# A two-block decoder kernel: first loads in one queue, a forget bias spread through HBM, and a recurrence whose second token block runs backwards

## The chip, the cores and the metric

The kernel runs on one core of a Trainium2 chip. The metric is the device time of one execution, in microseconds. The time before is 1769.55 us, the median of three runs (1769.51 to 1770.18).

Engines are named as the profile names them: PE (TensorE matmul), PEld (its weight load), DVE (VectorE), ACT (ScalarE), POOL (GpSimd) and SP (SyncE, which issues most DMAs). Each engine works through its own instructions in order; an instruction that waits for another engine holds up all that stand behind it.

## The reference, cut to what matters

256 tokens of width 2048 go through two residual blocks. The first has a gated linear recurrence (8 heads, 128 keys) beside dilated attention, then a convolution-gated MLP; the second has a causal convolution, attention with a forget gate, and memory attention. Only the recurrence and the forget bias are touched:

```python
q = silu(q_raw); f = lbh + (1 - lbh) * sigmoid(f_raw)
k = 1 - f; logf = log(f); v = i_raw
# S_t = diag(f_t) S_{t-1} + (1 - f_t) outer i_t ; o_t = S_t^T q_t
...
cT = cumsum(logf, axis=1).transpose(0, 2, 1)      # forget gate of the second block
bias = ci[..., :, None] - cT[..., None, :]
s = where(mask, q @ k.T * scale + bias, -inf)
```

The recurrence can be written as causal scores: the score of query t and key s is the sum over the 128 keys of q_t k_s times the product of all f between s and t.

## The kernel before

All activations lie as [feature, token] tiles in SBUF. Every large product is done in two parts: a weight piece is rounded to fp32r by ACT (`hi`, L208) and the rest is taken by DVE (`lo`, L193), and PE multiplies hi with both parts of the activation (L324, 512 columns) and lo with the first part (L326, 256 columns). One such pair is the beat of the kernel. `fm` makes [feature, token] outputs of 512 features in two halves of 16 k-tiles, 32 pairs each; `tm` makes [token, feature] outputs in 16 steps of six 512-column products (L389 to L391). SP streams the weights in the order of one list; a `raw` buffer is free again when its `lo` is made, and four pieces are kept ready ahead of PE.

The order of the instructions is written out by hand. `step()` (L287) is called after every second k-tile of `fm` and every k-tile of `tm`: it first does what has ended (`flush`: the evacuation of a half, `evac`, L360, and for a second half its `then`, such as `forgets`), and then lets the generator in the lane run to its next `yield`. So each `yield` of `hgrn` (L428) puts four pairs of `fm` (or six products of `tm`) between two of its stages.

`hgrn` treats four heads at a time and both blocks of 128 tokens. For levels L = 1, 2, 4 to 64, neighbouring stretches of L tokens are joined: PE multiplies all 128 keys of a block with all 128 of its queries (L455, 4 heads x 2 blocks = 8 products of 128 columns in full fp32), `copy_predicated` (L472) takes from the result the queries of the second stretch of each pair against the keys of the first, DVE multiplies these queries by the decay of the first stretch (L463), the keys of the first stretch by the decay of the second (L465), and the decays with one another (L468, `tot`). Then L477 multiplies the keys of block 0 with the queries of block 1, and L488 to L491 apply the scores to the values.

`forget` (L1073) ends with a cumulative sum `lz` of 8 rows; L1126 spreads each row over 128 partitions with a selector matrix, 16 fp32r products in four groups, and ACT and DVE carry them to `nb0` and `nb1`.

At the start, ACT issues the small `vec` and the first four k-tiles of x (L684, three transfers), SP the weights and the rest of x (`queue_first`, L236). `first` (L692) scales a k-tile (L152, L153) and then fetches its weight piece.

Of the kernel before, what the change touches and what calls it, by code (L numbers as in the profile page):

```python
# [17 lines left out]
T = 256  # L18
# [20 lines left out]
C_TRI, C_CAUS, C_LNC, C_LV = 0, 128, 256, 640  # L39
NCONST = 640 + 64 * len(LEVELS)  # L40


def constants():
    c = np.zeros((128, NCONST), np.float32)
    i = np.arange(128)
    c[:, C_TRI:C_TRI + 128] = i[:, None] <= i[None, :]
# [7 lines left out]
    for n, L in enumerate(LEVELS):  # L54
        t = i[i // L % 2 == 1]
        c[:, C_LV + 64 * n:C_LV + 64 * (n + 1)] = (i[:, None] // (2 * L) == t // (2 * L)) & (i[:, None] // L % 2 == 0)
    return c
# [10 lines left out]
def body(ctx: ExitStack, tc: tile.TileContext, A: dict, out: bass.AP):  # L68
# [10 lines left out]
    pb = ctx.enter_context(tc.tile_pool(name="pb", bufs=4, space=bass.MemoryType.PSUM))  # L79

# [346 lines left out]

    def hgrn(hh):  # L428
        f, q, v = hst.pop((hh, "f")), hst.pop((hh, "q")), hst.pop((hh, "v"))
        k = G("hk")  # L430
# [4 lines left out]
        Q = G("hQ")  # L435
        dve.tensor_tensor(out=Q, in0=q, in1=f, op=ALU.mult)
        yield
        for b in range(2):
            sl = slice(b * 128, (b + 1) * 128)
            ps = PB("sc", (128, 4, 128))  # L440
            for h in range(4):
                pe.matmul(ps[:, h, :], lhsT=k[:, h, sl], rhs=q[:, h, sl], start=True, stop=True)
            yield
            dve.tensor_tensor(out=SD[:, b], in0=ps, in1=bc(ident, 4), op=ALU.mult)
        yield
        tot = f.rearrange("p h t -> p (h t)")
        kf = k.rearrange("p h t -> p (h t)")
        Qf = Q.rearrange("p h t -> p (h t)")
        for n, L in enumerate(LEVELS):
            ps = []  # L450
            for b in range(2):
                sl = slice(b * 128, (b + 1) * 128)
                ps.append(PB("sc", (128, 4, 128)))
                for h in range(4):
                    pe.matmul(ps[b][:, h, :], lhsT=k[:, h, sl], rhs=Q[:, h, sl], start=True, stop=True)  # L455
            yield
            m = cst[:, C_LV + 64 * n:C_LV + 64 * (n + 1)].bitcast(U32).rearrange("p (n l) -> p n l", l=L)
            m = m.unsqueeze(1).to_broadcast([128, 4, 64 // L, L])
            Qv = Qf.rearrange("p (n a l) -> p n a l", a=2, l=L)[:, :, 1, :]
            kv = kf.rearrange("p (n a l) -> p n a l", a=2, l=L)[:, :, 0, :]  # L460
            tv = tot.rearrange("p (n a) -> p n a", a=2)
            t0, t1 = tv[:, :, 0], tv[:, :, 1]
            dve.tensor_tensor(out=Qv, in0=Qv, in1=bc(t0, L, 2), op=ALU.mult)  # L463
            yield
            dve.tensor_tensor(out=kv, in0=kv, in1=bc(t1, L, 2), op=ALU.mult)  # L465
            if L < 64:
                nt = G("tot", (128, 512 // L))
                dve.tensor_tensor(out=nt, in0=t0, in1=t1, op=ALU.mult)  # L468
                tot = nt
            yield  # L470
            for b in range(2):
                dve.copy_predicated(out=SD[:, b].rearrange("p h (n a l) -> p h n a l", a=2, l=L)[:, :, :, 1, :], mask=m,  # L472
                                    data=ps[b].rearrange("p h (n a l) -> p h n a l", a=2, l=L)[:, :, :, 1, :])
# [207 lines left out]
    with tc.manual_schedule():  # L681
        act.dma_start(out=vec[:, 0:16], in_=A["vecs"][:, 0:16])
        for a, b in ((0, 1), (1, 2), (2, 4)):
            act.dma_start(out=hT[0][:, a:b, :], in_=A["xT"][:, a:b, :])  # L684
# [7 lines left out]
        def first(rhs, src, name):  # L692
# [16 lines left out]
            for k0, n in FIRST:  # L709
                for k in range(k0, k0 + n):  # L710
                    rhs[k // 4].put_scaled(k % 4, src[k // 4][:, k % 4, :], V("ln_mix_pre", k))
                held.append(next_piece())
# [32 lines left out]

        def forgets(hh):
            def then(z):
                times(z, rb1)
                act.activation(out=z, in_=z, func=AF.Sigmoid)
                for h in range(4):  # L750
                    c = 4 * hh + h
                    dve.tensor_scalar(out=z[:, h, :], in0=z[:, h, :], scalar1=omlb[:, c:c + 1], scalar2=lb[:, c:c + 1],
                                      op0=ALU.mult, op1=ALU.add)
# [7 lines left out]
        silu(zq)  # L761
        hg = []
        for hh in range(2):
            hst[hh, "f"] = fm(uT, "hf", forgets(hh)) if hh else zf
            hst[hh, "q"] = fm(uT, "hq", silu) if hh else zq
            zf = zq = None
            if hh == 0:
                r1 = row_to_col(rb1, "r1")
            hst[hh, "v"] = token_scaled(tm(uT), r1, "hv")
# [298 lines left out]
        sel = G("sel", (8, 1024))  # L1068
        pool.dma_start(out=sel, in_=A["sel"])

        nbias = {}

        def forget():  # L1073
# [5 lines left out]
            s8 = G("selr", (8, 1024), F32R)  # L1079
            act.copy(out=s8, in_=sel)  # L1080
# [33 lines left out]
            c = Parts("nc", (8, T))  # L1114
            c.put(lz)
            yield
            yield
            caus = cst[:, C_CAUS:C_CAUS + 128]
            for hh in range(2):
                b0, b1 = G("nb0", (128, 4, 128)), G("nb1")  # L1120
                for p in range(2):
                    ps = PB("nb", (128, 2, T))
                    for a in range(2):
                        h = 4 * hh + 2 * p + a
# [4 lines left out]
                    hs = slice(2 * p, 2 * p + 2)  # L1129
                    act.copy(out=b1[:, hs, 0:128], in_=ps[:, :, 0:128])  # L1130
                    dve.tensor_tensor(out=b0[:, hs, :], in0=ps[:, :, 0:128], in1=bc(caus, 2), op=ALU.add)
                    dve.tensor_tensor(out=b1[:, hs, 128:256], in0=ps[:, :, 128:256], in1=bc(caus, 2), op=ALU.add)
                    yield
# [73 lines left out]
        del zp, zc, cu, sel  # L1207
# [99 lines left out]
```

## Time and profile before

| | |
|---|---|
| median of three runs | 1769.55 us |
| the profiled execution, device time | 1769.86 us |
| its span, first to last instruction | 1768.1 us |
| mean granted PE clock | 0.998 |
| DVE busy | 1191.6 us (67%) |
| ACT busy | 926.6 us (52%) |
| DMA | 323.73 MB, 183 GB/s in the mean |

The profile's share of busy time for PE counts products as pipelined, so that a single product's duration is longer than the distance to the next. What a group of products costs on PE is therefore read from the distance between starts. A row of the timeline gives the start, the duration, engine, line, operation, tiles and the number of records; a full fp32 product has two records, so "x16" on L455 are 8 products. In square brackets stands the idle time of that engine just before the row, and what ended it.

### The profile page before, as it was taken

How to read it: one execution, taken by the hardware profiler on the slowest of the kernel's cores; microseconds unless marked ns; L12 is line 12 of the kernel's file. 1: busy time of each engine (PE TensorE's matmuls, PEld its weight loads, DVE VectorE, ACT ScalarE, POOL GpSimd, SP SyncE). 2: the span in 40 equal slices, each digit the busy share in tenths (PEclk: the TensorE clock that was granted, in tenths of full speed). 3: DMA queues.
4: the chain of work that ended last, by engine and by line, in shares of the span. 5: the costliest groups of instructions: out<-in, count | busy, mean ns of one | idle time of the engine just before them, and what ended most of it. 6: DMA issues, size and time to landing. Idle time of an engine off the chain costs nothing.

```text
span 1768.1 us, 24303 instructions
## 1 busy us (share of the span) xinstructions
PE 1755.6 (99%) x9508; PEld 1513.0 (86%) x9508; DVE 1191.6 (67%) x1503; ACT 926.6 (52%) x1237; POOL 4.6 (0%) x12
## 2 busy tenths in 40 slices
PE   9999999999999999999999999999999999999998
PEld 8898988888888888888888888888888888888886
DVE  6775655567777777777777764444777688787564
ACT  6534354556655555555555653443655455448543
POOL 0000000000000000000000000000000000000000
PEclk9999999999999999999999999999999999999999
DMA  8644445555655665555565556555465545554553
GB/s 296 204 142 155 143 156 177 184 198 191 197 185 190 190 191 189 188 190 189 191 190 188 184 190 211 192 192 190 155 191 192 170 160 169 175 172 161 177 192 126
DMA packets 234482, 323.73 MB, mean 183 GB/s; under 512 B 10168, under 2 KB 203192, under 8 KB 234368
## 3 DMA queue, kind: packets, MB, share of 16 engines
q1 hardware_dynamic: 232816, 318.22, 55.2%
q0 software_dynamic: 976, 3.44, 0.6%
q8 instruction: 74, 1.21, 0.3%
q10 hardware_dynamic: 576, 0.53, 0.1%
q14 instruction: 40, 0.33, 0.1%
HBM read 320.06 MB, written 2.10 MB: 182 GB/s over the span
## 4 chain that ended last, share of the span: by engine, by line
PE 99%; DMA 0%; DVE 0%; ACT 0%; ACTq 0%; issue 0%; DVEq 0%
PE fm L324 40%; PE fm L326 20%; PE tm L389 10%; PE tm L390 10%; PE tm L391 10%; PE sc L455 1%; PE as L574 1%; PE fm L704 1%; PE ao L564 0%; DMA hT<-in_xT 0%; PE bd L623 0%; PE tm L1256 0%; PE tm L1254 0%; PE tm L1255 0%; PE at L553 0%; PE fm L705 0%
## 5 line engine op out<-in xcount | busy, mean ns | idle before, releaser
L324 PE MATMUL fm<-uT,hi 128*128 128x512 f32 x2688 | 947.9, 397 | 0.0
L208 ACT CAST hi<-raw 128x1024 fp32r<-128x1024 f32 (+1 forms) x591 | 617.1, 1048 | 590.6 <-PE fm L324 261.0
L193 DVE TENSOR_TENSOR lo<-raw,hi 128x1024 fp32r<-128x1024 f32 (+1 forms) x591 | 715.2, 1218 | 198.2 <-ACT hi L208 197.4
L326 PE MATMUL fm<-uT,lo 128*128 128x256 f32 x2688 | 747.9, 278 | 0.0
L324 PEld LDWEIGHTS fm<-uT,hi 128*128 128x128 f32 x2688 | 504.3, 188 | 116.2 <-issue 0.4
L326 PEld LDWEIGHTS fm<-uT,lo 128*128 128x128 f32 x2688 | 505.9, 188 | 0.9
L389 PE MATMUL tm<-hi,gp 128*128 128x512 f32 x352 | 136.9, 389 | 0.0
L391 PE MATMUL tm<-hi,gp 128*128 128x512 f32 x352 | 136.9, 389 | 0.0
L390 PE MATMUL tm<-lo,gp 128*128 128x512 f32 x352 | 136.9, 389 | 0.0
L363 DVE TENSOR_TENSOR up<-fm,up 128x512 f32<-128x512 f32 x44 | 30.4, 692 | 90.2 <-ACT up L362 89.3
L324 PE MATMUL fm<-hP,hi 128*128 128x512 f32 x256 | 90.7, 399 | 0.0
L391 PEld LDWEIGHTS tm<-hi,gp 128*128 128x128 f32 x352 | 66.1, 188 | 13.9
L390 PEld LDWEIGHTS tm<-lo,gp 128*128 128x128 f32 x352 | 66.1, 188 | 13.7
L389 PEld LDWEIGHTS tm<-hi,gp 128*128 128x128 f32 x352 | 66.1, 188 | 13.6
L880 ACT ACTIVATE upc<-up,vec 128x256 f32<-128x256 f32 x88 | 52.7, 599 | 45.9 <-DVE up L406 45.9
L389 PE MATMUL tm<-hi,uT 128*128 128x512 f32 x192 | 75.5, 393 | 0.0
L390 PE MATMUL tm<-lo,uT 128*128 128x512 f32 x192 | 74.9, 390 | 0.0
L391 PE MATMUL tm<-hi,uT 128*128 128x512 f32 x192 | 74.8, 389 | 0.0
L326 PE MATMUL fm<-hP,lo 128*128 128x256 f32 x256 | 71.9, 281 | 0.0
L324 PEld LDWEIGHTS fm<-hP,hi 128*128 128x128 f32 x256 | 48.1, 188 | 11.8
L1027 DVE SCALAR_TENSOR_TENSOR conv<-ca,vec,conv 128x255 f32<-128x255 f32 (+14 forms) x120 | 55.7, 464 | 1.5
L883 DVE SCALAR_TENSOR_TENSOR upc<-up,vec,upc 128x255 f32<-128x255 f32 x88 | 42.3, 480 | 14.1 <-ACT upc L880 14.1
(309 smaller groups left out, 1802.6 us busy)
## 6 DMA issues: line engine op xcount, KB each, us to landing
raw<-in_w_in SPq DMA_DIRECT2D x215, 512.0 KB, 4.6
raw<-in_w_up SPq DMA_DIRECT2D x176, 512.0 KB, 4.4
raw<-in_w_down SPq DMA_DIRECT2D x88, 512.0 KB, 4.5
raw<-in_w_out SPq DMA_DIRECT2D x64, 512.0 KB, 4.6
raw<-in_w_pg SPq DMA_DIRECT2D x32, 512.0 KB, 4.4
raw<-in_w_mem_kv SPq DMA_DIRECT2D x16, 512.0 KB, 4.8
memt<-in_memT POOLq DMA_DIRECT2D x4, 512.0 KB, 6.3
raw<-in_w_pe SPq DMA_DIRECT2D x4, 512.0 KB, 4.3
```

Source lines behind the costliest of these rows:

```text
L193: dve.tensor_tensor(out=lo, in0=src, in1=f32(hi), op=ALU.subtract)
L208: act.copy(out=hi, in_=src)
L324: pe.matmul(ps[:, f, :], lhsT=hi[:, kk, fs], rhs=u.both(i), start=(done == 0), stop=False, skip_group_check=True)
L326: pe.matmul(ps[:, f, T:2 * T], lhsT=lo[:, kk, fs], rhs=u.hi(i), start=False, stop=(done == n_k - 1), skip_group_check=True)
L363: dve.tensor_tensor(out=o, in0=ps[:, :, 0:T], in1=o, op=ALU.add)
L389: pe.matmul(ps[:, t, :], lhsT=u.hi(i)[:, ts], rhs=hi[:, kk, :], start=(done == 0), stop=False)
L390: pe.matmul(ps[:, t, :], lhsT=u.hi(i)[:, ts], rhs=lo[:, kk, :], start=False, stop=False)
L391: pe.matmul(ps[:, t, :], lhsT=u.lo(i)[:, ts], rhs=hi[:, kk, :], start=False, stop=(done == n_k - 1))
L455: pe.matmul(ps[b][:, h, :], lhsT=k[:, h, sl], rhs=Q[:, h, sl], start=True, stop=True)
L880: act.activation(out=y[:, f, :], in_=s[:, f, :], func=AF.Identity, scale=V("conv_w", 176 + c), bias=V("conv_b", c))
L883: dve.scalar_tensor_tensor(out=y[:, f, 1:], in0=s[:, f, 0:T - 1], scalar=V("conv_w", 88 + c), in1=y[:, f, 1:], op0=ALU.mult, op1=ALU.add)
L1027: dve.scalar_tensor_tensor(out=c[:, f, sh:], in0=cu[:, f, 0:T - sh], scalar=w, in1=c[:, f, sh:], op0=ALU.mult, op1=ALU.add)
```

## The change

- **First loads.** The three x transfers of ACT's queue are gone. SP now issues: weight tile 0, x tiles 0 and 1, weight tile 1, x tiles 2 and 3, weight tiles 2 and 3, and so on. `first` fetches the weight pieces 0 and 1 before it scales their x tiles.
- **Recurrence.** f, q, k and Q lie as [block, head, token], and block 1 has its tokens reversed. X holds, per head, one 128-column operand with the keys of the first stretches of block 0 and the second (in time: also first) stretches of block 1; Y holds the others. A level multiplies X with 64 queries of each block: 4 products of 128 columns, with a right operand read in runs of L. After the product, ACT copies half of X from Y, and DVE makes the other half of X, `tot` and half of Y. One more `yield` stands ahead of the levels, with two ACT copies that build X and Y. The values of block 1 are reversed by three POOL transfers through HBM.
- **Forget bias.** The selector, its load and L1126 go. POOL writes `lz` to HBM, reads four rows at a time back to all 128 partitions, and after eight yields DVE adds the causal mask.

```diff
     def queue_first(w, c0):
         for k, n in FIRST:
-            if k in (4, 8, 12):
-                load_x(k, k + 4)
+            if k in (2, 4, 8, 12):
+                load_x(k, min(2 * k, k + 4))
...
+            if k == 0:
+                load_x(0, 2)
...
     def hgrn(hh):
...
+        scores = (SD[:, 0], SD[:, 1, :, ::-1])
...
+        X2, Y = G("hX", (128, 2, 512)), G("hY", (128, 512))
+        X = X2[:, 0]
+        act.copy(out=X.rearrange("p (n a) -> p n a", a=2), in_=strided(kf, 0, (2, 256), (513, 2)))
+        act.copy(out=Y.rearrange("p (n a) -> p n a", a=2), in_=strided(kf, 512, (2, 256), (-511, 2)))
+        del k, kf
+        yield
+        for e, (L, masks) in enumerate(zip(LEVELS, C_LV)):
+            ps = PB("sc", (128, 4, 2, 64))
+            for h in range(4):
+                pe.matmul(ps[:, h].rearrange("p b q -> p (b q)"), lhsT=X[:, h * 128:(h + 1) * 128],
+                          rhs=strided(Qf, h * 128 + L, (512 - L, 2), (2 * L, 64 // L), (1, L)), start=True, stop=True)
+            yield
+            N, S = 256 // L, 512 // L
+            Qv = strided(Qf, L, (512 - L, 2), (2 * L, N), (1, L))
+            dve.tensor_tensor(out=Qv, in0=Qv, in1=strided(tot, 0, (S + 1, 2), (2, N), (0, L)), op=ALU.mult)
+            yield
+            X1 = X2[:, 1 - e % 2]
+            if L < 64:
+                M = N // 2
+                same, other = ((4 * L, M), (3 * L, 2), (1, L)), ((4 * L, M), (L, 2), (1, L))
+                act.copy(out=strided(X1, L, *other), in_=strided(Y, L, *other))
+                dve.tensor_tensor(out=strided(X1, 0, *same), in0=strided(X, 0, *same),
+                                  in1=strided(tot, 1, (4, M), (S + 1, 2), (0, L)), op=ALU.mult)
...
             yield
...
         ps = PB("sc", (128, 4, 128))
         for h in range(4):
-            pe.matmul(ps[:, h, :], lhsT=k[:, h, 0:128], rhs=Q[:, h, 128:256], start=True, stop=True)
-        act.copy(out=SO, in_=ps)
+            pe.matmul(ps[:, h, :], lhsT=X[:, h * 128:(h + 1) * 128], rhs=Q[:, 1, h, :], start=True, stop=True)
+        act.copy(out=SO[:, :, ::-1], in_=ps)
...
         act.dma_start(out=vec[:, 0:16], in_=A["vecs"][:, 0:16])
-        for a, b in ((0, 1), (1, 2), (2, 4)):
-            act.dma_start(out=hT[0][:, a:b, :], in_=A["xT"][:, a:b, :])
...
+        def folded(z, func, name):
+            y = G(name, (128, 2, 4, 128))
+            act.activation(out=y[:, 0], in_=z[:, :, 0:128], func=func)
+            act.activation(out=y[:, 1], in_=z[:, :, 255:127:-1], func=func)
+            return y
...
         def forgets(hh):
             def then(z):
                 times(z, rb1)
-                act.activation(out=z, in_=z, func=AF.Sigmoid)
+                y = folded(z, AF.Sigmoid, "hf")
...
+            pool.dma_start(out=rows, in_=v[:, 1, :])
...
+            pool.dma_start(out=back.rearrange("t (a c) -> a t c", a=2),
+                           in_=rows[::-1, :].rearrange("t (a c) -> a t c", a=2))
+            pool.dma_start(out=v[:, 1, :], in_=back)
...
-                        for part in (c.hi, c.lo):
-                            pe.matmul(ps[:, a, :], lhsT=s8[:, 128 * h:128 * (h + 1)], rhs=part, start=(part is c.hi),
-                                      stop=(part is c.lo))
...
+            pool.dma_start(out=spread, in_=lz)
...
+                pool.dma_start(out=b1, in_=spread[4 * hh:4 * hh + 4, :].partition_broadcast(128))
+                for _ in range(8):
                     yield
```

Three places of the order matter for what follows. The first is DVE in the recurrence of the first four heads, around level 4, where the second half of the next f (`hf`) is evacuated (L363), scaled by the norm (L406) and turned into f (L752). Before:

```order
L463 TENSOR_TENSOR hQ<-hQ,tot 128x128x4
L465 TENSOR_TENSOR hk<-hk,tot 128x128x4
L468 TENSOR_TENSOR tot<-tot 128x128
L193 TENSOR_TENSOR lo<-raw,hi 128x1024
L363 TENSOR_TENSOR hf<-fm,hf 128x512
L406 TENSOR_TENSOR hf<-hf,rb 128x1024
L752 TENSOR_SCALAR hf<-hf,omlb,lb 128x256 x4
L472 COPY_PREDICATED SD<-cst,sc 128x64x4 x2
L193 TENSOR_TENSOR lo<-raw,hi 128x1024
```

The same place on DVE now (L367, L410 and L784 are the evacuation, the norm and f; L480 makes X):

```order
L473 TENSOR_TENSOR hQ<-hQ,tot 128x2x64x4
L195 TENSOR_TENSOR lo<-raw,hi 128x1024
L367 TENSOR_TENSOR hf<-fm,hf 128x512
L410 TENSOR_TENSOR hf<-hf,rb 128x1024
L784 TENSOR_SCALAR hf<-hf,omlb,lb 128x2x128 x4
L480 TENSOR_TENSOR hX<-hX,tot 128x32x2x4
L484 TENSOR_TENSOR tot<-tot 128x128
L485 TENSOR_TENSOR hY<-hX,tot 128x32x8
L497 COPY_PREDICATED SD<-cst,sc 128x64x4
L497 COPY_PREDICATED SD<-cst,sc 128x4x16x4
```

Before, the keys for level 8 (L465) stood ahead of the work on f; now X for level 8 (L480) stands behind it.

The second place is ACT at the end of the same recurrence, at level 64, where the second half of the next q (`hq`) gets its Silu and the last product's result is copied to SO. Before:

```order
L362 COPY hq<-fm 128x512
L758 ACT_TABLE_LOAD
L758 ACTIVATE hq<-hq 128x1024
L478 COPY SO<-sc 128x512
L208 CAST hi<-raw 128x1024 x2
```

Now (L479 and L489 are the copies from Y to X):

```order
L479 COPY hX<-hY 128x4x64
L210 CAST hi<-raw 128x1024 x2
L366 COPY hq<-fm 128x512
L774 ACT_TABLE_LOAD
L774 ACTIVATE hq<-hq 128x512
L775 ACTIVATE hq<-hq 128x512
L489 COPY hX<-hY 128x4x64
L210 CAST hi<-raw 128x1024
L503 COPY SO<-sc 128x4x128
```

A copy that the last product needs now stands behind the table load and the Silu.

The third place is SP's first DMAs. Before (row 1 is two transfers, and ACT's three x transfers go out beside them):

```order
L185 DMA raw<-in_w_in 128x512 x2
L185 DMA raw<-in_w_in 128x1024
L229 DMA hT_89<-in_xT 128x1024
L185 DMA raw<-in_w_in 128x1024 x2
L229 DMA hT_90<-in_xT 128x1024
```

Now:

```order
L187 DMA raw<-in_w_in 128x512
L231 DMA hT_90<-in_xT 128x512
L187 DMA raw<-in_w_in 128x512
L231 DMA hT_90<-in_xT 128x512
L187 DMA raw<-in_w_in 128x1024
L231 DMA hT_91<-in_xT 128x1024
L187 DMA raw<-in_w_in 128x1024 x2
```

All of x's first tiles stand in the one queue, each beside the weights that meet it.

## Rows read from the trace of the kernel before

**Rows 1.** The page's first part: busy time, share of the span and instructions of each engine.

```profile
PE 1755.6 (99%) x9508; PEld 1513.0 (86%) x9508; DVE 1191.6 (67%) x1503; ACT 926.6 (52%) x1237; POOL 4.6 (0%) x12
```

**Rows 2.** All waits of PE over the span: waiting engine and line, what it waited for, us in total, times, longest us. There are five; the three left out are one wait each of under 1.2 us, none of them in the recurrence.

```profile
PE fm L704 <- DVE uT L153: 1.9, 1, 1.9
...
PE fm L705 <- DVE lo L193: 0.6, 1, 0.6
```

**Rows 3.** The timeline of PE in the recurrence of the first four heads: start us, duration us, engine, line, operation. Between 81.47 and 83.77 lie four pairs of L324 and L326, between 89.57 and 94.43 fourteen, between 87.44 and 94.78 sixteen.

```profile
81.47 1.05 PE L442 MATMUL sc<-hq,hk 128*128 128x128 f32 x8
...
83.77 1.05 PE L442 MATMUL sc<-hq,hk 128*128 128x128 f32 x8
...
87.44 1.95 PE L455 MATMUL sc<-hQ,hk 128*128 128x128 f32 x16
...
89.57 0.40 PE L324 MATMUL fm<-uT,hi 128*128 128x512 f32 x1
...
94.43 0.39 PE L324 MATMUL fm<-uT,hi 128*128 128x512 f32 x1
...
94.78 1.95 PE L455 MATMUL sc<-hQ,hk 128*128 128x128 f32 x16
```

**Rows 4.** The timeline of PE at the first two groups of the forget bias; eight pairs lie between the groups, six of them between 1436.39 and 1438.51.

```profile
1435.28 0.73 PE L1126 MATMUL nb<-nc,selr 8*128 8x256 f32 x4
...
1436.39 0.39 PE L324 MATMUL fm<-uT,hi 128*128 128x512 f32 x1
...
1438.51 0.40 PE L324 MATMUL fm<-uT,hi 128*128 128x512 f32 x1
...
1438.95 0.74 PE L1126 MATMUL nb<-nc,selr 8*128 8x256 f32 x4
```

**Rows 5.** The first 12 us in stretches: its length, busy us (and instructions) of PE, PEld, DVE, ACT and POOL, granted PE clock, DMA share, GB/s.

```profile
0.00:4.00 4.00, 2.95 (x14) 2.95 (x15) 0.17 (x2) 1.36 (x2) 0.20 (x4) 1.00 0.34 78
4.00:6.00 2.00, 1.56 (x10) 1.37 (x9) 0.00 (x0) 0.11 (x1) 0.00 (x0) 1.00 1.01 369
6.00:8.00 2.00, 0.47 (x1) 0.19 (x1) 1.13 (x2) 1.01 (x2) 0.00 (x0) 1.00 1.02 406
8.00:10.00 2.00, 1.90 (x6) 1.70 (x7) 1.20 (x3) 1.02 (x2) 0.00 (x0) 0.56 1.04 395
10.00:12.00 2.00, 2.00 (x9) 1.67 (x8) 0.91 (x3) 1.86 (x4) 0.00 (x0) 0.59 1.03 414
```

**Rows 6.** The start of the chain that ended last: start us, us, what. The first row is the transfer of x tiles 2 and 3.

```profile
2.15 7.97 DMA hT<-in_xT
10.14 0.91 ACT uT L152 x2
...
12.02 1.24 DVE lo L193
```

**Rows 7.** The timeline of PE at the first product, at a later pair, and at the product that the last row of the group before releases.

```profile
7.48 0.47 PE L704 MATMUL fm<-uT,hi 128*128 128x512 f32 x1 [1.92 <-DVE uT L153]
...
9.02 0.63 PE L704 MATMUL fm<-uT,hi 128*128 128x512 f32 x1
...
9.66 0.63 PE L704 MATMUL fm<-uT,hi 128*128 128x512 f32 x1
...
13.30 0.38 PE L705 MATMUL fm<-uT,lo 128*128 128x256 f32 x1 [0.58 <-DVE lo L193]
```

**Rows 8.** The timelines of ACT, DVE and PE where the second half of `hf` ends, by engine.

```profile
110.40 1.06 ACT L749 ACTIVATE hf<-hf 128x1024 f32<-128x1024 f32 x1 [0.71 <-DVE hf L406]
...
111.49 1.38 DVE L752 TENSOR_SCALAR hf<-hf,omlb,lb 128x256 f32<-128x256 f32 x4 [1.12 <-ACT hf L749]
112.78 0.76 DVE L472 COPY_PREDICATED SD<-cst,sc 128x256 f32<-128x256 uint32 x2
...
109.54 1.95 PE L455 MATMUL sc<-hQ,hk 128*128 128x128 f32 x16
```

**Rows 9.** The same where the second half of `hq` ends: PE's first product of `tm` behind it and the product that stands 12 products later, and ACT's Silu.

```profile
136.21 0.39 PE L389 MATMUL tm<-hi,uT 128*128 128x512 f32 x1
...
138.98 1.05 PE L477 MATMUL sc<-hQ,hk 128*128 128x128 f32 x8
...
139.84 1.06 ACT L758 ACTIVATE hq<-hq 128x1024 f32<-128x1024 f32 x1 [0.72 <-DVE hq L406]
```

**Rows 10.** The same place as rows 8 for the other four heads, where the half is of `aq` and only scaled.

```profile
193.53 1.23 DVE L406 TENSOR_TENSOR aq<-aq,rb 128x1024 f32<-128x1024 f32 x1
...
193.94 1.95 PE L455 MATMUL sc<-hQ,hk 128*128 128x128 f32 x16
```

**Rows 11.** Durations of DVE and ACT work on 256 and 512 columns: a group of DVE by form (busy us, mean ns), the copies of ACT at L1130, and the multiply of the queries at levels 2 to 64 and at level 1 (ns min/median/max).

```profile
L468 DVE TENSOR_TENSOR tot<-tot 128x256 f32<-128x256 f32 x1 | 0.4, 417 | 0.0
...
L1130 ACT COPY nb<-nb x4: 352/364/374, 1436.5 to 1447.4; 128x256 f32<-128x256 f32 x4
...
L463 DVE TENSOR_TENSOR hQ<-hQ,tot x12: 683/692/694, 96.8 to 218.0; 128x512 f32<-128x512 f32 x12
L463 DVE TENSOR_TENSOR hQ<-hQ,hf x2: 693/694/695, 89.4 to 173.8; 128x512 f32<-128x512 f32 x2
```

**Rows 12.** POOL's transfers: size, us from issue to landing. `gf` is one row spread over 128 partitions.

```profile
gf<-in_final_g POOLq DMA_DIRECT2D x2, 512.0 KB, 5.2
...
sel<-in_sel POOLq DMA_DIRECT2D x1, 32.0 KB, 3.1
```

More of the change, by code (lines that the diff above doesn't have):

```diff
@@ L37 @@
 NVEC = _o
-C_TRI, C_CAUS, C_LNC, C_LV = 0, 128, 256, 640
-NCONST = 640 + 64 * len(LEVELS)
+C_CAUS, C_LNC = 0, 128
+C_LV = [(512 + 128 - 128 // L, 512 + 127 + 128 - 128 // L) for L in LEVELS]
+NCONST = 512 + 2 * 127
 def constants():
@@ L445, in hgrn @@
         yield
[L446 to L455, printed above, removed]
-            yield
[L457 to L463, printed above, removed]
+        tot = f.rearrange("p b h t -> p (b h t)")
@@ L467, in hgrn @@
                 nt = G("tot", (128, 512 // L))
-                dve.tensor_tensor(out=nt, in0=t0, in1=t1, op=ALU.mult)
+                tv = tot.rearrange("p (n a) -> p n a", a=2)
+                dve.tensor_tensor(out=nt, in0=tv[:, :, 0], in1=tv[:, :, 1], op=ALU.mult)
+                dve.tensor_tensor(out=strided(Y, L, *other), in0=strided(X, L, *other),
+                                  in1=strided(tot, S, (4, M), (3 - S, 2), (0, L)), op=ALU.mult)
                 tot = nt
+            else:
+                act.copy(out=strided(X1, 64, (128, 4), (1, 64)), in_=strided(Y, 64, (128, 4), (1, 64)))
+                dve.tensor_tensor(out=strided(X1, 0, (128, 4), (1, 64)), in0=strided(X, 0, (128, 4), (1, 64)),
+                                  in1=strided(tot, 1, (2, 4), (0, 64)), op=ALU.mult)
@@ L748, in then, with queries @@
                 times(z, rb1)
-                act.activation(out=z, in_=z, func=AF.Sigmoid)
+                y = folded(z, AF.Sigmoid, "hf")
                 for h in range(4):
                     c = 4 * hh + h
-                    dve.tensor_scalar(out=z[:, h, :], in0=z[:, h, :], scalar1=omlb[:, c:c + 1], scalar2=lb[:, c:c + 1],
-                                      op0=ALU.mult, op1=ALU.add)
+                    dve.tensor_scalar(out=y[:, :, h, :], in0=y[:, :, h, :], scalar1=omlb[:, c:c + 1],
+                                      scalar2=lb[:, c:c + 1], op0=ALU.mult, op1=ALU.add)
+                hst[hh, "f"] = y
+            return then
+        def queries(hh):
+            def then(z):
+                times(z, rb1)
+                hst[hh, "q"] = folded(z, AF.Silu, "hq")
             return then
@@ L760, in body @@
         forgets(0)(zf)
-        silu(zq)
+        queries(0)(zq)
+        del zf, zq
         hg = []
         for hh in range(2):
[L764 to L767, printed above, removed]
+            if hh:
+                fm(uT, "hf", forgets(hh))
+                fm(uT, "hq", queries(hh))
+            else:
                 r1 = row_to_col(rb1, "r1")
-            hst[hh, "v"] = token_scaled(tm(uT), r1, "hv")
+            v = token_scaled(tm(uT), r1, "hv")
+            rows = dp.tile([128, 512], F32, name="rows")
+            pool.dma_start(out=rows, in_=v[:, 1, :])
+            back = dp.tile([128, 512], F32, name="back")
+            pool.dma_start(out=back.rearrange("t (a c) -> a t c", a=2),
+                           in_=rows[::-1, :].rearrange("t (a c) -> a t c", a=2))
+            pool.dma_start(out=v[:, 1, :], in_=back)
+            hst[hh, "v"] = v
+            del v
             join(*hg)
@@ L1067, in body @@
         tg = spawn(token_major())
-        sel = G("sel", (8, 1024))
-        pool.dma_start(out=sel, in_=A["sel"])
         nbias = {}
@@ L1113, in forget @@
                     yield
-            c = Parts("nc", (8, T))
-            c.put(lz)
-            yield
+            spread = dp.tile([8, T], F32, name="spread")
+            pool.dma_start(out=spread, in_=lz)
             yield
@@ L1120, in forget @@
                 b0, b1 = G("nb0", (128, 4, 128)), G("nb1")
[L1121 to L1124, printed above, removed]
-                        for part in (c.hi, c.lo):
-                            pe.matmul(ps[:, a, :], lhsT=s8[:, 128 * h:128 * (h + 1)], rhs=part, start=(part is c.hi),
-                                      stop=(part is c.lo))
-                    yield
[L1129 to L1133, printed above, removed]
+                pool.dma_start(out=b1, in_=spread[4 * hh:4 * hh + 4, :].partition_broadcast(128))
+                for _ in range(8):
+                    yield
+                dve.tensor_tensor(out=b0, in0=b1[:, :, 0:128], in1=bc(caus, 4), op=ALU.add)
+                dve.tensor_tensor(out=b1[:, :, 128:256], in0=b1[:, :, 128:256], in1=bc(caus, 4), op=ALU.add)
+                yield
                 nbias[hh] = (b0, b1)
@@ L1206, in body @@
         yg[0] = spawn(conv_out(zp, zc))
-        del zp, zc, cu, sel
+        del zp, zc, cu
         del uT
```

37 lines of the change are left out of this document (22 added, 15 removed).

## The prediction

> **What bounds the kernel now.** I read the page's first part, then the waits of PE, then the timelines of the three places that the change touches. PE has work for 1755.6 of 1768.1 us [rows 1], and it waits almost nowhere: the two waits that the change can touch are 1.9 and 0.6 us at the first products, and none lies in the recurrence [rows 2]. So a product taken from PE is worth what it takes in PE's row, and a wait put ahead of a product costs its full length, since nothing else can pass it on PE. The other engines have room; what they do counts only where PE stands waiting. The sum is made against the profiled execution (1769.86 us, 0.3 above the median of 1769.55).
>
> **Recurrence, the products removed.** A pair of L324 and L326 takes (94.43 - 89.57) / 14 = 0.347 us. From one L455 group to the next pass 7.34 us, with sixteen pairs: 5.55, so eight fp32 products cost 1.78 us. Whether four cost half is seen at L442: 2.30 us between groups of four, less four pairs (1.39), is 0.91, so there is no price per group beside the products [rows 3]. Now each level has four in place of eight: 0.89 us less, times 7 levels, times 2 halves of the heads = **12.5 us**. The right operand is now read in runs of L with gaps. No row shows PE reading so. Bounds: no cost, or half speed, which takes four products back to 1.78 us and the whole 12.5 with it. I take no cost, by the nearest row, DVE's multiply of the queries: at level 1, where it reads and writes every second float, it takes 693 to 695 ns, at levels 2 to 64 683 to 694 [rows 11]. The last product (L477) and the score products keep their count.
>
> The Trainium skill (Advanced Engine Details and Errata, SBUF Cachelines) says that accesses which stay twice in a 16-byte line run at full speed and that a new line at each access is punished. By it PE's operand is free at all levels (every second float at level 1 is two per line), but `tot` as X's factor at level 1 steps four floats, one per line; doubling that one multiply (0.42 us) would put it 0.4 us later. No run here shows it.
>
> **Recurrence, the new wait.** The extra `yield` moves every level's product by four pairs against the halves of `fm`. It now stands twelve pairs behind the end of a half, and X is issued behind the work that this end sets off (the DVE and ACT places shown under the change). Before, the keys were multiplied ahead of that work.
>
> At level 8 of the first heads: L455 starts at 109.54 and stands eight pairs behind the half's end, so that is 109.54 - 2.78 = 106.76. In the new order the product is due twelve pairs behind it: 106.76 + 4.17 = 110.93. But f is ready only when L752 hands over to the next work on DVE, at 112.78 [rows 8]; X follows with 256 columns, 0.42 us [rows 11]: 113.2. The two Sigmoids of 512 columns for one of 1024 may add 0.1. PE waits 2.3 us.
>
> At the last product: `hq` ends with 136.21, twelve `tm` products take 138.98 - 136.21 = 2.77, so eighteen take 4.15 and the product is due at 140.36. Silu begins at 139.84 and lasts 1.06 [rows 9]; behind it ACT copies half of X, 256 columns, 0.36 [rows 11]: 141.26. PE waits 0.9 us.
>
> For the other four heads only the scaling stands between: L406 ends at 193.53 + 1.23 = 194.76, X 0.42 later at 195.2, and the product is due at 193.94 - 2.78 + 4.17 = 195.33 [rows 10]. No wait, by 0.15 us; the same holds at its end. Where a first half ends, only the evacuation stands there, and X is in time. Together **+3.2 us**; bounds: 0, if X is made earlier than I read, and about 6, if Y, reversed reading and the two halves of X add 0.7 at each of the four places. What is queued behind the late X on DVE are splits of weights that PE needs four pieces later; they are not late.
>
> The rest of the recurrence's DVE and ACT work (per level X and Y with 256 columns each for keys with 512, two more 256-column copies on ACT) lies beside at least sixteen pairs, 5.55 us; DVE is busy 67% of the span, ACT 52% [rows 1]. If that cover is gone it costs PE at each level: a rival, below. The reversal of the values is issued some 60 us before the product that reads it; three POOL transfers at 3 to 5 us each [rows 12] are 15 at most.
>
> **Forget bias.** From group to group 1438.95 - 1435.28 = 3.67 us, with eight pairs of (1438.51 - 1436.39) / 6 = 0.353: 2.83. So a group of four costs 0.85 us, and four groups **3.4 us** (lower bound: the durations shown, 0.73 less overlap, 0.66 x 4 = 2.6) [rows 4]. In its place `lz` goes to HBM (3.1 us like `sel`) and comes back over 128 partitions (5.2 like `gf`) [rows 12]: 8.3 us. DVE's add stands nine steps behind, nine times four pairs = 12.7 us. It costs nothing; if DVE had to wait there for 2 or 3 us, the four pieces ahead (32 pairs, 11 us) cover PE.
>
> **First loads.** Today x tiles 2 and 3 are asked for at 2.15 and land 7.97 us later; with the cast and the split behind it PE goes on at 13.30 [rows 6, 7]. By rows 5, 312 KB have moved by 4 us, 1050 by 6, 1862 by 8, 2652 by 10. Each transfer is 8 chunks for each of 16 engines; if the two queues take turns chunk by chunk, that x transfer goes out beside the fourth of SP, when 520 + 1536 = 2056 KB have moved, at 8.5 us, and counts as landed 1.6 later. In one queue, weight tiles 2 and 3, the last data that k-tile 2 needs, stand behind 1544 KB: 7.2 us, landed 8.8 (estimate from these rows). Cast 1.0, split 1.24 and the order on DVE make 11.2. PE itself begins at about 7.2 (x tiles 0 and 1 at 520 KB: 4.6 + 1.6, then scaling) and has eight pairs to do. Before, PE stood idle from 5.6 to 7.48, and its granted clock was 0.56 and 0.59 from 8 to 12 us, mostly 1.2 GHz: a pair took 0.64 [rows 5, 7]. If the clock falls again at the same time, the eight pairs end at 11.4 and the gain is 1.65; if not, 2.1. I take **1.7 us**; bounds 0 and 2.5.
>
> The trace's turns between two queues go against leaving x on ACT. The Trainium skill (DMA: Bandwidth & Descriptors, Issuing engines are not separate DMA queues) speaks against the merge: all queues run on the same engines, so a second issuer saves issue time only, and that saving is now given up. SP then issues weight tiles 2 and 3 two issues of 0.43 us later; by that alone the gain would shrink to about 0.8 us and the sum come out at 1756.1. The DMA share of 1.01 from 4 us on [rows 5] says that data, not issue, is short.
>
> **Sum.** 12.5 + 3.4 + 1.7 - 3.2 = 14.4. 1769.86 - 14.4 = 1755.5; against the median 1755.2 us.
>
> **Rivals.**
> - *No new wait.* X is in time everywhere, all else as above: 1752.0. For it: PE has hardly a wait now. Against: the chain of rows 8 is 1.9 us too long even without X. 20%.
> - *The gapped operand is slow where the runs are short.* At levels 1 and 2 products at half speed: 2 x 0.89 x 2 = 3.6 us back, 1758.8. 12%. At all levels: 12.5 back, 1767.7, within what a measurement can tell from no change. 5%. For it: no row shows such a read on PE; against: DVE's level 1.
> - *A late transfer.* The forget bias or the values land so late that DVE outlasts the pieces ahead, some us: about 1762. 4%.
> - *Slower.* At each level PE waits for X. The chain behind a product is the multiply of the queries 0.69, a split 1.24, X 0.42: 2.4 us against 5.55 of cover. From 5.55 on each us costs 14 (7 levels, twice); from 6.6 on the kernel is slower, at 7 it is 1755.2 + 20 = 1775. That takes gapped DVE and ACT work at about three times its rows, against the 693 to 695 ns of level 1. 4%.
>
> **How the numbers follow.** My forecast has 55%, its own range is 1752.5 to 1758.5. About 0.2% (3.5 us) is what a measurement of this kernel can tell from no change. Faster by more: all cases but the operand that is slow at all levels (5%, within it) and the last one (4%, slower), so 91%. The range 1750 to 1761 takes in the rival without a wait, the slow short runs, and the ends of the first loads and the waits (12.5 + 3.4 + 2.5 = 18.4 below; 12.5 + 2.6 + 0 - 6 = 9.1 above).
>
> **What would show it.** In the profile after: the group of the level products with 112 records for 224, and level to level 6.4 us for 7.34; a wait of PE for hX on DVE of some 2.3 us at level 8 of the first heads and for hX on ACT of some 0.9 at the last product, none at the others; no PE row for `nb`; PE's first product near 7.2 and its k-tile 2 near 11.4. It is wrong if pairs beside the levels grow, if a group of four takes much over 0.9 us at levels 1 and 2, or if PE waits at levels that follow no end of a half.

## The result, and the profile after

The changed kernel takes 1758.41 us (median of 6 runs, 1757.42 to 1759.16), beside 1770.24 for the kernel before on the same chip (6 runs, 1769.51 to 1771.58). The ratio is 0.9932, with a 95% interval of 0.9920 to 0.9943: faster by 11.8 us. The forecast of 1755.2 asked for 14.4; the result lies in its range of 1750 to 1761, and at the upper end of the narrower one, 1752.5 to 1758.5. In the profiled execution (1757.93 us, span 1756.2) the span is 11.9 us shorter. What has to be explained is not a large miss, but where 2.6 us of the expected gain went.

The first part of the page, which answers to [rows 1]:

```profile
PE 1742.2 (99%) x9380; PEld 1500.4 (85%) x9380; DVE 1191.7 (68%) x1510; ACT 935.1 (53%) x1253; POOL 10.2 (1%) x20
```

PE has 128 instructions fewer (9508 to 9380): 112 in the recurrence and 16 of the forget bias. PE's busy time falls by 13.4 us and the span by 11.9, so there are new idle stretches. (Beside the three parts listed under the change, the table of constants is smaller: its transfer is 383 KB for 544. No term was set for it.) The waits of PE name them (engine and line that waits, what it waited for, us in total, times, longest us), to be held against [rows 2]:

```profile
PE sc L468 <- DVE hX L480: 2.4, 1, 2.4
...
PE sc L502 <- ACT hX L489: 0.9, 1, 0.9
PE fm L727 <- DVE uT L155: 0.6, 1, 0.6
```

These are the two waits that the forecast named, at the two places it named and with its sizes (2.3 and 0.9 us), and no third one in the recurrence. The start waits 0.6 us for the first scaled tile in place of 1.9.

The timeline of PE in the recurrence of the first four heads, all level products and the last one (start, duration, line, operation; in brackets the idle time before it and its releaser). It answers to [rows 3]; sixteen pairs lie from one group to the next:

```profile
79.78 1.05 PE L452 MATMUL sc<-hq,hk 128*128 128x128 f32 x8
...
87.13 1.07 PE L468 MATMUL sc<-hQ,hX 128*128 128x128 f32 x8
93.59 1.07 PE L468 MATMUL sc<-hQ,hX 128*128 128x128 f32 x8
100.05 1.05 PE L468 MATMUL sc<-hQ,hX 128*128 128x128 f32 x8
109.06 1.59 PE L468 MATMUL sc<-hQ,hX 128*128 128x128 f32 x8 [2.40 <-DVE hX L480]
117.16 1.05 PE L468 MATMUL sc<-hQ,hX 128*128 128x128 f32 x8
123.61 1.05 PE L468 MATMUL sc<-hQ,hX 128*128 128x128 f32 x8
130.05 1.05 PE L468 MATMUL sc<-hQ,hX 128*128 128x128 f32 x8
137.53 1.16 PE L502 MATMUL sc<-hQ,hX 128*128 128x128 f32 x8 [0.91 <-ACT hX L489]
...
238.66 1.05 PE L599 MATMUL as<-ak,aq 128*128 128x128 f32 x8
```

The reader sees three things. Level to level takes about 6.45 us where nothing waits, against 7.34 before; that is the expected 0.89 per level. From the third group to the fourth it takes 9.01, which holds the wait. And from the fourth to the fifth it takes 8.10, although the fifth group waits for nothing. This last stretch was in no term of the forecast. The same place in stretches of 1 us (length; PE's busy time and instructions; granted clock; DMA share; GB/s):

```profile
108.00:109.00 1.00, 0.00 (x0) 1.00 0.00 0
109.00:110.00 1.00, 0.94 (x6) 0.78 0.00 0
110.00:111.00 1.00, 1.00 (x6) 0.50 0.00 0
111.00:112.00 1.00, 1.00 (x5) 0.50 0.07 16
112.00:113.00 1.00, 1.00 (x4) 0.51 0.57 205
113.00:114.00 1.00, 1.00 (x7) 1.00 0.76 274
```

PE stands still from 106.66 to 109.06. While it does, the record reads 1.00; it falls in the stretch in which PE works again. From then on the granted clock is 0.50, that is 1.2 GHz in place of 2.4, until about 113, and the pairs there take 0.64 us for 0.347, as PE's timeline shows:

```profile
111.09 0.63 PE L328 MATMUL fm<-uT,hi 128*128 128x512 f32 x1
...
111.73 0.63 PE L328 MATMUL fm<-uT,hi 128*128 128x512 f32 x1
```

The second wait, 0.91 us before 137.53, leaves the clock at 1.00. Read in stretches of 20 us over the kernel, the clock of this execution is under 1.00 in one of them only, 100 to 120 us.

Why X is late at that level is read on DVE (same columns):

```profile
104.75 1.22 DVE L410 TENSOR_TENSOR hf<-hf,rb 128x1024 f32<-128x1024 f32 x1
107.20 1.38 DVE L784 TENSOR_SCALAR hf<-hf,omlb,lb 128x256 f32<-128x256 f32 x4 [1.22 <-ACT hf L775]
108.49 0.42 DVE L480 TENSOR_TENSOR hX<-hX,tot 128x256 f32<-128x256 f32 x1
```

It is the chain of [rows 8], half on ACT and half on DVE, that ends a half of `hf`, with X queued behind it.

At the forget bias no `nb` product is left on PE, and the stretch from the product with `pick` to the next layer's first score product shrinks. First the kernel before, then the changed one:

```profile
1419.56 0.59 PE L1097 MATMUL fl<-lz,pick 16*8 16x256 f32 x2
...
1467.50 1.05 PE L574 MATMUL as<-fk,fq 128*128 128x128 f32 x8
```

```profile
1410.84 0.59 PE L1140 MATMUL fl<-lz,pick 16*8 16x256 f32 x2
...
1455.35 1.05 PE L599 MATMUL as<-fk,fq 128*128 128x128 f32 x8
```

47.94 us become 44.51, a gain of 3.43 us.

### The profile page after: what moved, and what is told of

Its sections match the earlier page's. It is cut to its first block, busy times and chain, and to the rows that moved or that the text cites. A ratio compares the mean times of both kernels' runs of the same rounds, so it can differ in the third digit from the quotient of the medians.

```text
span 1756.2 us, 24083 instructions
## 1 busy us (share of the span) xinstructions
PE 1742.2 (99%) x9380; PEld 1500.4 (85%) x9380; DVE 1191.7 (68%) x1510; ACT 935.1 (53%) x1253; POOL 10.2 (1%) x20
## 4 chain that ended last, share of the span: by engine, by line
PE 93%; DVE 0%; ACT 0%; issue 0%; DVEq 0%; ACTq 0%
PE fm L328 38%; PE fm L330 19%; PE tm L393 10%; PE tm L394 10%; PE tm L395 10%; PE as L599 1%; PE sc L468 1%; PE ao L589 0%; PE bd L648 0%; PE tm L1291 0%; PE tm L1290 0%; PE tm L1289 0%; PE at L578 0%; PE fm L351 0%; PE fm L354 0%; PE fm L353 0%
## 5 line engine op out<-in xcount | busy, mean ns | idle before, releaser
L367 DVE TENSOR_TENSOR up<-fm,up 128x512 f32<-128x512 f32 x44 | 30.4, 692 | 89.9 <-ACT up L366 89.0
L328 PEld LDWEIGHTS fm<-hP,hi 128*128 128x128 f32 x256 | 48.1, 188 | 11.8
```

What stands on the lines that cost most here:

```text
L328: pe.matmul(ps[:, f, :], lhsT=hi[:, kk, fs], rhs=u.both(i), start=(done == 0), stop=False, skip_group_check=True)
L367: dve.tensor_tensor(out=o, in0=ps[:, :, 0:T], in1=o, op=ALU.add)
```

## The experiments

All were timed against the kernel before on their own chip: 1770.20 us in the first four, 1769.92 in the other four. "The recurrence's stretch" is the time on PE from the first product of L452 (L442 before) to the first score product of the attention heads, `as<-ak,aq`. Before, that is 247.43 - 81.47 = 165.96 us; in the changed kernel 238.66 - 79.78 = 158.88, so 7.08 less. It holds everything of the recurrence and nothing of the start, and is read from one trace, which makes it sharper than the totals. The first score product of the attention heads in the kernel before, in PE's timeline:

```profile
247.43 1.05 PE L574 MATMUL as<-ak,aq 128*128 128x128 f32 x8
```

**The extra step taken out.** In `hgrn`, the step between the multiplies of the scores and ACT's copies of X and Y goes:

```diff
             dve.tensor_tensor(out=scores[b], in0=ps, in1=bc(ident, 4), op=ALU.mult)
-        yield
```

> The changed kernel with one line moved: the yield behind the two ACT copies that build X and Y is gone, so that every level's product stands four pairs earlier and X is issued ahead of the work on the next f and q. Theory A (what is missing of the gain is the two waits of PE for X, 2.4 and 0.9 us, and about 1.7 us in which PE ran its products at half speed after the first wait): no wait of PE for hX, level to level 6.45 us everywhere, 1758.4 - 5.0 = 1753.4 us. Theory B (only the waits cost; the other 1.9 us that the recurrence of the first heads lost lie in products that became slower beside the gapped operand and the new copies): 1758.4 - 3.3 = 1755.1 us, with the slow pairs still there.

(The expectation speaks of the `yield` behind the two copies; the one taken out is the neighbour ahead of them, as the diff shows. The products stand four pairs earlier by either.)

Measured: 1753.47 us (4 runs, 1752.49 to 1753.54), ratio 0.9904 (0.9888 to 0.9921). No wait for `hX` is left, and the timeline of PE shows 6.44 to 6.55 us from level to level:

```profile
80.83 1.05 PE L452 MATMUL sc<-hq,hk 128*128 128x128 f32 x8
...
99.72 1.05 PE L467 MATMUL sc<-hQ,hX 128*128 128x128 f32 x8
106.16 1.05 PE L467 MATMUL sc<-hQ,hX 128*128 128x128 f32 x8
112.71 1.05 PE L467 MATMUL sc<-hQ,hX 128*128 128x128 f32 x8
...
132.09 1.05 PE L501 MATMUL sc<-hQ,hX 128*128 128x128 f32 x8
...
234.28 1.05 PE L598 MATMUL as<-ak,aq 128*128 128x128 f32 x8
```

The recurrence's stretch is 153.45 us, 12.51 less than before: the forecast's 12.5 for the products removed, complete. So what the changed kernel loses of it, 158.88 - 153.45 = 5.43 us, all comes with the one extra step, where the forecast had put 3.2. It can be followed in the two timelines. From the third level group to the fifth the changed kernel takes 117.16 - 100.05 = 17.11 us and this one 112.71 - 99.72 = 12.99: the first wait costs 4.12, not 2.40. From the fifth to the last product it is 20.37 against 19.38: the second wait costs 0.99. That makes 5.11. Of the other 0.3, 0.19 lies in the other four heads: no wait is recorded there, but at level 8 and at the last product X is ready only as PE's weight load for it begins, and these two groups last 1.09 and 1.13 us for 1.05. The rest stays without a name. This kernel is also the fastest of the study.

**The first wait filled with products.** Before the level product at 8 of the first four heads PE computes products of ones, whose result nobody reads: 20 instructions in the first kernel (ten fp32 products), 10 in the second. X is as late as before; only PE's idle time differs.

```diff
+            if hh == 0 and L == 8:
+                keep_warm(10)
```

> The changed kernel with ten products of ones (about 0.224 us each, 2.2 us) ahead of the level-8 product of the first heads, into the wait of 2.4 us; the wait itself stays. Theory A (the idle stretch lets PE's clock fall): the granted clock stays at 1.00 through the following 4 us, a pair takes 0.347 us, the time is 1758.4 - 1.7 = 1756.7 us. Theory B (the slow pairs have nothing to do with PE standing idle): 1758.4 us and the pairs at 0.63 us again.

> The same with five products of ones (1.1 us), so that PE still stands idle for some 1.3 us. Theory A with an idle stretch of 1.3 us being short enough, as the 0.9 us at the last product was: 1756.7 us, clock 1.00. Theory A with 1.3 us being long enough, as the 2.4 us was: 1758.4 us, clock 0.5 for some us. Theory B: 1758.4 us.

Measured: 1757.40 us (1756.58 to 1758.03, ratio 0.9928, 0.9913 to 0.9943) and 1757.39 (1756.45 to 1758.03, the same ratio). The totals lie 1.0 under the changed kernel's median, between the two theories, and their intervals overlap its own; by them alone nothing is settled. The traces do it. With ten products, timeline of PE:

```profile
107.55 2.39 PE L705 MATMUL warm<-ones 128*128 128x128 f32 x20
110.11 1.13 PE L470 MATMUL sc<-hQ,hX 128*128 128x128 f32 x8 [0.17 <-DVE hX L482]
116.73 1.05 PE L470 MATMUL sc<-hQ,hX 128*128 128x128 f32 x8
```

With five, the same view, and then the stretches behind it:

```profile
107.97 1.28 PE L705 MATMUL warm<-ones 128*128 128x128 f32 x10
110.53 1.13 PE L470 MATMUL sc<-hQ,hX 128*128 128x128 f32 x8 [1.29 <-DVE hX L482]
117.15 1.05 PE L470 MATMUL sc<-hQ,hX 128*128 128x128 f32 x8
```

```profile
111.00:112.00 1.00, 1.00 (x9) 1.00 0.08 16
112.00:113.00 1.00, 1.00 (x8) 1.00 0.00 0
```

The product comes 2.56 us after the filling begins in both (107.55 to 110.11, 107.97 to 110.53), and 9.00 us after the third group, no earlier than in the changed kernel (9.01), so the wait itself is still paid. But the next level follows after 6.62 us in place of 8.10, with the clock at 1.00. So the idle 2.4 us had a second price, 8.10 - 6.62 = **1.48 us of half clock behind it**, and an idle stretch of 1.29 us at the same place had none, in one execution of each. The recurrence's stretch is 238.48 - 80.83 = 157.65 and 238.80 - 81.25 = 157.55 us, 1.2 to 1.3 less than the changed kernel's. The rest of the 1.48 is lost in the next two levels, which take 6.55 and 6.54 us here and 6.45 and 6.44 in the changed kernel; distances of either size stand in the other traces too, and why isn't known.

**The operand without gaps.** The kernel without the extra step, with PE's right operand read in one run of 128. The scores are then those of other queries; the amount of work is the same.

```diff
-                          rhs=strided(Qf, h * 128 + L, (512 - L, 2), (2 * L, 64 // L), (1, L)), start=True, stop=True)
+                          rhs=Q[:, 0, h, :], start=True, stop=True)
```

> The kernel of e1 with the right operand of the level products read without gaps (the 128 queries of block 0 in a row instead of the gapped queries of both blocks, so these scores are those of other queries). If PE reads the gapped operand at full speed: the same time as e1 within 0.5 us, a group of four at 0.89 to 0.91 us in both. If short runs cost at levels 1 and 2: up to 3.6 us faster than e1.

Measured: 1753.66 us (1753.43 to 1753.79), against 1753.47 with the gaps. In the changed kernel the groups at levels 1 and 2 last 1.07 us and the others 1.05 (the timeline above); without gaps all last 1.05. So the gapped operand in runs of one and two floats costs PE 0.02 us a group, and nothing that the total shows.

**One part of the change alone.** First the kernel before with the first loads in one queue and nothing else:

```diff
-            if k in (4, 8, 12):
-                load_x(k, k + 4)
+            if k in (2, 4, 8, 12):
+                load_x(k, min(2 * k, k + 4))
...
+            if k == 0:
+                load_x(0, 2)
...
-        for a, b in ((0, 1), (1, 2), (2, 4)):
-            act.dma_start(out=hT[0][:, a:b, :], in_=A["xT"][:, a:b, :])
```

> The kernel before with the merged first loads and nothing else of the change. Theory A (the forecast's term, and what the profiled execution of the changed kernel shows, the first recurrence product 1.69 us earlier): 1.7 us faster, about 1768.5. Theory B (that execution was lucky: in four later profiled ones the same product starts at 80.83 to 81.25 us against 81.47, since TensorE at full clock catches up with the 512 KB x load behind it, which lands 8.7 to 10.8 us after its issue): 0.2 to 0.7 us faster, about 1769.7, with one wait of TensorE for the fourth piece's lo. Theory C (nothing or a loss): 1770.2 or above.

Measured: 1768.93 us (11 runs, 1768.55 to 1770.07), beside 1769.92 (21 runs). The medians differ by 1.0; the ratio of 0.9996 has an interval of 0.9988 to 1.0005, which holds no change too. Nine of the eleven are shorter than the shortest of the 21, so a gain is likely, and its size is between A and B. The profiled execution is the slowest of the eleven. Its timeline of PE shows a wait at the third piece (k-tile 2) and, as B has it, one at the fourth (k-tile 4):

```profile
11.46 0.38 PE L705 MATMUL fm<-uT,lo 128*128 128x256 f32 x1 [0.77 <-DVE lo L193]
15.46 0.39 PE L705 MATMUL fm<-uT,lo 128*128 128x256 f32 x1 [0.76 <-DVE lo L193]
```

Then the forget bias alone, in the kernel before:

```diff
-                for p in range(2):
-                    ps = PB("nb", (128, 2, T))
...
+            spread = dp.tile([8, T], F32, name="spread")
+            pool.dma_start(out=spread, in_=lz)
...
+                pool.dma_start(out=b1, in_=spread[4 * hh:4 * hh + 4, :].partition_broadcast(128))
```

> The kernel before with the forget bias over HBM and nothing else of the change. Theory A (32 products of 0.1 us leave TensorE and nothing takes their place): 3.4 us faster, about 1766.8, and the stretch from the lz,pick product to the first score product of the forget layer 3.44 us shorter in the trace. Theory B (the broadcast transfer is late without the changed recurrence ahead of it): under 2 us faster, with a wait of VectorE or TensorE at the bias.

Measured: 1766.57 us (11 runs, 1765.68 to 1767.23), ratio 0.9980 (0.9971 to 0.9988): 3.35 faster. In the timeline of PE the stretch is 1464.45 - 1419.95 = 44.50 us, as in the changed kernel:

```profile
1419.95 0.59 PE L1093 MATMUL fl<-lz,pick 16*8 16x256 f32 x2
...
1464.45 1.05 PE L575 MATMUL as<-fk,fq 128*128 128x128 f32 x8
```

**The fastest kernel with the old loads.** The kernel without the extra step, with the first loads undone (the diff of the first loads above, backwards).

> The kernel of e1_no_extra_step with the first loads of the kernel before. The forget bias (3.4) and the recurrence without a wait (12.5) alone, with A (loads worth 1.7): 1755.2. With B (loads worth 0.2 to 0.7): 1753.7 to 1754.2. With C: 1753.4 or less, and then the old loads are the better ones. In all of them the stretch from the first recurrence product to the first score product of the attention heads is 153.4 us as in e1_no_extra_step, against 165.96 before.

Measured: 1754.42 us (5 runs, 1753.93 to 1754.74), ratio 0.9913 (0.9899 to 0.9927). The recurrence's stretch is 235.54 - 82.09 = 153.45, equal to that with the new loads. Against 1753.47 the new loads are worth 0.95 here, and 1.2 if each kernel is taken against the kernel before on its own chip (15.5 and 16.7 us faster); both are over what B allows. Its start repeats what [rows 5] showed; PE stood 2.7 us idle and began at 8.85, and the stretches read:

```profile
9.00:11.00 2.00, 1.85 (x7) 0.78 1.01 402
11.00:13.00 2.00, 2.00 (x8) 0.50 1.04 418
```

**The changed kernel once more**, unaltered, beside the last three.

> The changed kernel once more, beside the three others. A: its start as profiled (first recurrence product at about 79.8 us), total 1758.0. B: the product at 80.8 to 81.3 in most executions, total 1758.2 to 1759.2. In both the 2.4 us wait for hX at the fourth level comes with a fall of the granted clock to 0.5 for about 3 us behind it, and the stretch from the first recurrence product to the attention heads is 158.9 us.

Measured: 1758.31 us (5 runs, 1757.05 to 1758.37), ratio 0.9933 (0.9921 to 0.9946). Timeline of PE:

```profile
80.09 1.05 PE L452 MATMUL sc<-hq,hk 128*128 128x128 f32 x8
...
109.37 1.18 PE L468 MATMUL sc<-hQ,hX 128*128 128x128 f32 x8 [2.40 <-DVE hX L480]
117.52 1.05 PE L468 MATMUL sc<-hQ,hX 128*128 128x128 f32 x8
```

Again 2.40 us of wait and 8.15 us to the next group (granted clock 0.58 and 0.57 from 110 to 114). So the loss behind the wait is no accident of one execution. The recurrence's stretch is 239.04 - 80.09 = 158.95. The start, 80.09, is early again, as A has it, yet the total is B's.

## Why the prediction was right, and by what it was off

By its own terms, with what the runs put in their place:

| term | forecast | measured | from |
|---|---|---|---|
| recurrence, products removed | -12.5 | -12.5 | stretch 165.96 to 153.45 without the extra step |
| forget bias | -3.4 | -3.35 | that part alone; 3.43 in the trace |
| first loads | -1.7 | -1.0 | that part alone (its interval holds 0); 0.95 to 1.2 undone |
| the new waits | +3.2 | +5.4 | the extra step taken out; 5.1 of it at the two waits |
| sum | -14.4 | -11.5 | -11.8 and -11.6 timed |

**Products removed: right.** Level to level about 6.45 for 7.34 us, at every level without a wait, in the trace of the changed kernel and of the kernel without the step. A group of four fp32 products costs half of eight, as the difference between L442 and L455 had said.

**Forget bias: right.** The group price from the distance of two groups (0.85) and not from the durations (0.66) was the one to take. The transfers are hidden: `lz` lands after 1.8 us and the broadcast after 6.0 (5.2 was taken from `gf`), and DVE's add waits for nothing.

**The new waits: the places and the lengths were right, the price was wrong.** The step that failed is "a wait put ahead of a product costs its full length", with "PE waits 2.3 us" as the whole cost at level 8. The wait is 2.40 us; it cost 4.12. Of this, 2.57 is how much later the product starts than 6.44 us behind the group ahead, where it was due (the 2.40 of idle time count from the end of the product ahead, and the filling could begin at 6.44); 1.48 is the half clock behind it, and 0.07 is left over. The second wait cost 0.99 for 0.91. The forecast could have had this: [rows 5] and [rows 7] show the same thing at the start of the kernel before, where PE idles 1.92 us and then runs at 0.56 and 0.59 with pairs of 0.64. It was used there, in the term on the first loads, and not applied to the wait that the change itself brings. Four microseconds at a clock of 0.56 to 0.59, as there, lose 4 x 0.42 = 1.7; with that the forecast would have been 1756.9.

**The other four heads: right.** No wait at any of their levels or at their last product, as the 0.15 us in hand had it; the list of waits has none. It was close: X ends 0.12 us before the weight load at both places (189.70 and 189.82, 215.74 and 215.86), and the two groups are 0.04 and 0.08 us longer than the others.

**First loads: the direction was right, the size was not.** The step that failed is the chain that took one place, k-tile 2, for the whole start. At that place the gain came as forecast. In the profiled execution of the changed kernel the product that [rows 7] show at 13.30 stands at 11.60, and the first product of the recurrence comes 1.69 us earlier:

```profile
11.60 0.28 PE L728 MATMUL fm<-uT,lo 128*128 128x256 f32 x1
```

In the kernel with the loads alone it stands at 11.46, 1.84 us earlier than before. But there PE ran the first pairs at full speed and stands again at the next piece: the product at 15.46 was at 16.18 before, so 0.72 of the gain is left, and at the recurrence none (81.59 against 81.47). Over seven profiled executions with the new loads the recurrence begins at 79.78 to 81.59 us (mean 80.75), over three with the old ones at 81.47 to 82.09 (mean 81.80): 1.05 us, as the totals say, though with so few executions whose ranges touch the size is a rough one. The data are what is short for some pieces yet: ACT's casts ahead of the products at 11.46 and 15.46 wait for their weights' transfer (0.73 us before 9.10, 0.37 before 13.10). A gain at one piece is partly taken back at the next. That the two queues took turns before was worked out from one landing time; no run tests it. The objection that the prediction drew from the Trainium skill (DMA: Bandwidth & Descriptors, Issuing engines are not separate DMA queues: issuing from several engines saves issue time only) would have left 0.8 of the 1.7. Its number is nearer than the forecast's. Its reason isn't shown by these runs: with the loads alone, the DMA share is 0.94 to 1.02 in the four stretches of 2 us from 5 to 13 us, which speaks for data being short and not its issue; no run moved the issues by themselves.

**The rivals.** "No new wait" fell in the changed kernel, and taking the step out made it true: 1753.47, against the 1752.0 that it gave; 0.7 of the difference is the first loads, and 0.65 that the kernel before ran at 1770.20 beside it and not at 1769.55. "The gapped operand is slow where the runs are short" gave 1758.8, nearest of all to the 1758.4 that was measured, and is false: the groups at levels 1 and 2 last 1.07 us for 1.05, and without gaps the total stays. A total that agrees proves no mechanism; the row of the group does. "A late transfer": the values' reversal takes three transfers of 3.9, 9.4 and 3.9 us, 17 in place of "15 at most", and is still done well before the product that reads it. "Slower": no level waits for X except where a half ends.

## What to carry to other kernels

A wait has a price behind it as well as its length. Where the profile shows that a pause of TensorE was followed by a granted clock at the lower level, price every new wait of that length with it: here 2.40 us of idle time cost 4.12, of which 1.48 lay behind the wait, while 0.91 cost 0.99. Where such a wait can't be taken away, products of no use in its idle time keep the clock, and win back only the second part.

Where work is merged into fewer products whose operand has to be prepared, the place of the preparation in the order decides: one `yield` put it behind the end of another projection's half, and cost 5.4 of the 12.5 us that the merge had brought. A single step less gave all of it back.

Price a change at the start over several profiled executions: with the same first loads the same product began up to 1.8 us apart, which is more than the term that was asked for.

## What the runs showed of the hardware

- Idle time of PE and the granted clock behind it: 1.92 us (before, start), 2.40 us (twice, at the level product) and 2.74 us (the old loads in the fastest kernel) were each followed by stretches between 0.50 and 0.59; 0.91 us at the last product, 1.20 us at the start of the kernel with the forget bias alone, and 1.29 us with five filling products were followed by 1.00. At the level product the clock fell only when PE was at work again. Most of these are single executions, and the next point is one that their order by length doesn't cover.
- In the profiled execution of the changed kernel, the pairs of the first products stand 0.64 us apart up to 10.67 us, while the granted clock reads 1.00 there, and PE had been idle for only 0.60 us before them. This is the timeline of PE, and the stretch:

```profile
8.80 0.63 PE L727 MATMUL fm<-uT,hi 128*128 128x512 f32 x1
...
9.44 0.63 PE L727 MATMUL fm<-uT,hi 128*128 128x512 f32 x1
```

```profile
8.00:10.00 2.00, 2.00 (x8) 1.00 0.97 315
```

  The second execution of the same kernel starts with pairs at full speed. Why, and whether the record of the clock missed a fall, stays open.
- PE reads every second float at no price to speak of (0.02 us in a group of 1.05). DVE does pay at level 1 of X, where its factor steps four floats. By groups of lines from 78 to 200 us of the changed kernel (busy us, mean ns; the first row is the other levels, the second level 1):

```profile
L480 DVE TENSOR_TENSOR hX<-hX,tot 128x256 f32<-128x256 f32 x8 | 3.4, 419 | 0.0
...
L480 DVE TENSOR_TENSOR hX<-hX,hf 128x256 f32<-128x256 f32 x2 | 1.3, 634 | 0.0
```

  That is half as long again, 0.22 us; Y at level 1 (L485) pays the same, 642 ns for 421. The Trainium skill (Advanced Engine Details and Errata, SBUF Cachelines) states a penalty for a different cacheline at each access and gives no size; the 0.4 of the prediction was an estimate by doubling. The direction agrees, and it is hidden here. At level 1 X and its result too are touched in runs of one float, so these rows don't show which operand pays.
- Reversing the rows of 256 KB from HBM to HBM through POOL's queue took 9.4 us, more than twice the plain transfers of the same data beside it (3.9), which go between SBUF and HBM. No run separates the reversal from the way from HBM to HBM.
